# State-space parameter work of a decoder block cut into shorter pieces, all on VectorE, at six points of a pair of feature blocks

## The chip, the cores and the metric

The kernel runs on one core of a Trainium2 chip. The metric is the device time of one execution in microseconds (us), from the profiler's clock of that core; lower is better. Three executions of the kernel before are given, and one more was profiled.

## What is computed

One layer of a decoder block over 1024 tokens of width 1024, in fp32: a SwiGLU feed-forward (inner width 2816), a token mixer (a gated short convolution beside a diagonal state-space scan), a second SwiGLU, and a gated embedding, each followed by a layer norm. Cut to what the change touches:

```python
def swiglu(x, w_in, w_out):
    gate, up = jnp.split(x @ w_in, 2, axis=-1)
    return (jax.nn.silu(gate) * up) @ w_out

def s5_scan(u, lam_re, lam_im, log_step, b_re, b_im, c_re, c_im, d_skip):
    lam = lax.complex(lam_re, lam_im)
    dt = jnp.exp(log_step)[:, None]
    lam_bar = jnp.exp(lam * dt)
    b_bar = ((lam_bar - 1.0) / lam)[..., None] * b_c
...
```

The scan's parameters (powers of lam_bar, b_bar, and the products that the blocked scan multiplies with) depend on small inputs alone. They are computed on the chip while the first feed-forward runs, and stored for the mixer.

## The kernel before, in words

Every fp32 matmul is made of three passes over values split into a high part (fp32r, rounded by ScalarE, L175) and a low part (the rest, subtracted by VectorE, L176). A weight block 128x512 so becomes the tiles Wh and Wl, in a ring of three buffers each.

The first feed-forward (`ffn`, L470) goes through 22 feature blocks, each a `Pair` of a gate half and an up half, over two halves of the tokens. A Winograd scheme needs seven products per pair instead of eight: x11, t1, t2, t3, x21, x22, t4, in that order on TensorE, each of 4 x 3 = 12 matmuls of 512 columns (L198). Three of the seven weight operands come straight from HBM (`Ws`); the other four are sums and differences that GpSimd forms (L79, L84, L88, L96), three of them in the one tile `s` that is written again as soon as its last split has read it. VectorE adds the products in `Pair.rest` (L87, L92, L99, L101, all with one operand in PSUM) and multiplies gate and up (L494, L495). For every second pair GpSimd (L533, L535) and VectorE (L537, L539) also form four sums for the output product.

Between these steps `ffn` draws pieces of a generator, `ssm_prep` (L729): at a point, `tick` runs the generator to its next `yield`, and what it issues is placed after the instruction of that point. The first five pairs have no points. Fifteen pairs have three points each (L87, L99, L495), 45 in all, and the generator has 40 pieces. At the end of the fifteenth the rest of it would be run off, the residual input is loaded (L1155), and the two last pairs and the output product follow.

`ssm_prep` begins with some 150 small operations on 16 to 128 elements per partition (exponentials, sine and cosine, powers; L658 to L807), all on VectorE. Then come four quarters, each with three outer products of complex numbers, `outer`, of 128x512 elements: L, CP and rot, each six operations in `cmul` (L722 to L727, four products, then two sums). L is formed by GpSimd, CP and rot by VectorE. After them TensorE transposes L (L859, 8 transposes), ScalarE scales CP into a block (L846, four operations), and small matmuls (L872, L875) go out through VectorE and ScalarE (L876, L878). The next quarter loads its own small inputs into the one buffer `bc` (L815).

All instructions of an engine run in one order, which the scheduler of the framework writes down from its own estimate of times. So a piece lies on VectorE's queue ahead of or behind the splits that TensorE needs next.

Of the kernel before, what the change touches and what calls it, by code (L numbers as in the profile page):

```python
# [28 lines left out]
class Pair:  # L29
# [43 lines left out]
    def rest(self, tick=lambda ins: None):  # L73
        blk = self.blk
        nc, gps, vec = blk.nc, blk.nc.gpsimd, blk.nc.vector
        u2 = self.u2
        a11, a21, a22 = self.w(0), self.w(0, 1), self.w(1, 1)
        s = blk.t("Ws", [P, 512], name="s")
        gps.tensor_tensor(s, a21, a22, ALU.add)  # L79
        b3 = blk.pm()  # L80
        self.prod(b3, s, "t1")
        p5 = blk.t("T", [P, 512], name="p5")
        nc.scalar.copy(p5, b3)
        gps.tensor_tensor(s, s, a11, ALU.subtract)  # L84
        b2 = blk.pm()
        self.prod(b2, s, "t2")
        tick(vec.tensor_tensor(u2, b2, u2, ALU.add))  # L87
        gps.tensor_tensor(a21, a11, a21, ALU.subtract)  # L88
        b4 = blk.pm()
        self.prod(b4, a21, "t3")  # L90
        u3 = blk.t("T", [P, 512], name="u3")
        vec.tensor_tensor(u3, b4, u2, ALU.add)  # L92
        a12 = self.w(1)
        if not self.early:
            self.second()
        gps.tensor_tensor(s, a12, s, ALU.subtract)  # L96
        self.prod(b3, s, "22", start=False)
        self.a2 = blk.t("H", [P, 512], name="a2")
        tick(vec.tensor_tensor(self.a2, b3, u2, ALU.add))  # L99
        self.prod(b4, a22, "t4", start=False)  # L100
        vec.tensor_tensor(u2, b4, u2, ALU.add)  # L101
        gps.tensor_tensor(u3, u3, p5, ALU.add)  # L102
        self.c1, self.c2 = u2, u3


class Block:
# [363 lines left out]
    def ffn(self, xs, w_in, w_out, acc, after, between, points, begun=(None, None), ahead=None, at=None, early=None):  # L470
        staged, later = begun
        nc = self.nc
# [10 lines left out]
        def products(p):  # L483

            marks = iter(range(points if not p.early else 0))

            def tick(ins):
                if next(marks, None) is not None:
                    with self.tc.issue_after(ins.ins):
                        next(between, None)  # L490

            p.rest(tick)
            nc.scalar.activation(p.a2, p.a2, AF.Silu)
            vec.tensor_tensor(p.a1, p.a1, p.c1, ALU.mult)  # L494
            tick(vec.tensor_tensor(p.a2, p.a2, p.c2, ALU.mult))  # L495
            return p.a1, p.a2

# [154 lines left out]
    def exp_small(self, out, x, n, tmp):  # L652
# [8 lines left out]
        v.scalar_tensor_tensor(r, k, -0.693359375, xc, ALU.mult, ALU.add)  # L661
        v.scalar_tensor_tensor(r, k, 2.12194440e-4, r, ALU.mult, ALU.add)
        v.tensor_scalar(p, r, 1.0 / 5040, None, ALU.mult)
        for c in (1.0 / 720, 1.0 / 120, 1.0 / 24, 1.0 / 6, 0.5, 1.0):
            v.scalar_tensor_tensor(p, p, c, r, ALU.add, ALU.mult)
        v.tensor_scalar(p, p, 1.0, None, ALU.add)
        v.tensor_scalar(k, k, 127.0, None, ALU.add)
        v.tensor_copy(ki, k)
# [3 lines left out]
    def sincos_small(self, sn, cs, x, n):  # L672
# [32 lines left out]
        v.tensor_tensor(c, c, o, ALU.mult)  # L705
        v.tensor_tensor(sn, sn, s, ALU.add)
        v.tensor_tensor(cs, c, w, ALU.add)

        v.tensor_scalar(o, q, 2.0, None, ALU.is_ge)
        v.tensor_scalar(o, o, -2.0, 1.0, ALU.mult, ALU.add)  # L710
# [18 lines left out]
    def ssm_prep(self, prm, dsk, prm_bc):  # L729


        nc = self.nc
        v, gps = nc.vector, nc.gpsimd
        G = 16
        self.scratch = self.carve(self.r("RR", [P, D], 3))
        keep = self.carve(self.r("prm", [P, 368], 1))
# [6 lines left out]
        self.exp_small(dt, lst, G, "e1")  # L743
# [6 lines left out]
        self.exp_small(mag, e2, 2 * G, "e2")  # L750
        yield
        yield from self.sincos_small(sn, cs, th2, 2 * G)
        yield
# [7 lines left out]
        def powers(x, n):  # L761

            v.memset(x[0][:, :, 0:1], 1.0)
            v.memset(x[1][:, :, 0:1], 0.0)
            m = 1
            while m < n:
                br, bi = (y[:, :, m:m + 1].broadcast_to([P, G, m]) for y in x)
                self.cmul(v, x[0][:, :, m + 1:2 * m + 1], x[1][:, :, m + 1:2 * m + 1],
                          x[0][:, :, 1:m + 1], x[1][:, :, 1:m + 1], br, bi, t0[:, :, :m], t1[:, :, :m])
                m *= 2  # L770

        v.tensor_tensor(pw[0][:, :, 1:2], mag[:, :G].unsqueeze(2), cs[:, :G].unsqueeze(2), ALU.mult)
        v.tensor_tensor(pw[1][:, :, 1:2], mag[:, :G].unsqueeze(2), sn[:, :G].unsqueeze(2), ALU.mult)
        powers(pw, 8)
        yield
# [27 lines left out]
        powers(zp, 16)  # L803
        yield
        for ri in range(2):
            v.tensor_copy(wp[ri][:, :, 1:2], zp[ri][:, :, 16:17])
        powers(wp, 8)  # L807
        yield
        for q in range(4):
            g0 = 4 * q  # L810
            gs = slice(g0, g0 + 4)
# [8 lines left out]
            self.cmul(v, bb[0], bb[1], bc[:, 0], bc[:, 1],  # L820
                      *(x[:, gs].unsqueeze(2).broadcast_to([P, 4, 16]) for x in (qr, qi)), t0, t1)

            def outer(eng, dst, x, y):

                xr, xi = (a.unsqueeze(3).broadcast_to(B4) for a in x)
                yr, yi = (a.unsqueeze(2).broadcast_to(B4) for a in y)
                t0, t1 = self.t("T", B4), self.t("T", B4)
                self.cmul(eng, dst[:, 0], dst[:, 1], xr, xi, yr, yi, t0, t1)

            yield  # L830
            L = self.r("RR", [P, 2, 4, 8, 16], 3)
            outer(gps, L, [a[:, gs, 0:8] for a in pw], bb)
            yield
            CP = self.r("RR", [P, 2, 4, 8, 16], 3)
            outer(v, CP, [a[:, gs, 1:9] for a in pw], cc)
            yield

            rot = self.r("RS", [P, 2, 4, 8, 16], 2)
            outer(v, rot, [a[:, gs, 0:8] for a in wp], [a[:, gs, 0:16] for a in zp])
            nc.sync.dma_start(self.rot_d[q], rot.rearrange("p c g a b -> p (c g a b)"))  # L840
            yield

# [297 lines left out]
    def run(self, a, out):  # L1140
# [22 lines left out]
        def then(acc, make, sink):  # L1163
# [3 lines left out]
            def after(s):  # L1167
# [4 lines left out]
                if s % 2:  # L1172
# [4 lines left out]


        state, after = then(acc, self.new_xs, lambda x: self.winograd_sink(x, gbT[0]))
        self.ffn(xs, a["ffn1_w_in"], a["ffn1_w_out"], acc, after, prep(), 3, begun,  # L1180
                 at=19, early=start)

        acc2, last = self.mixer(state["x"], a, acc)
# [129 lines left out]
```

## Time and profile before

| what | value |
|---|---|
| median of 3 runs | 2100.65 us (2095.39 to 2104.41) |
| the profiled execution | 2100.17 us, its span 2098.3 us |
| TensorE busy | 2006.1 us, 96% of the span |
| VectorE busy | 1657.9 us, 79% |
| GpSimd busy | 884.9 us, 42% |
| ScalarE busy | 813.1 us, 39% |
| mean granted TensorE clock | 0.989 of full speed |

The span runs from the first to the last instruction. PE is the matmul side of TensorE, PEld its weight loads, DVE VectorE, ACT ScalarE, POOL GpSimd, SP the engine whose queue issues the DMAs. The generator's pieces lie from about 124 us to 412 us of the span, inside the first feed-forward's pairs.

### The profile page before, as it was taken

The numbers are of one execution on the slowest core, as the hardware profiler recorded it, in microseconds if no ns is written. First come the engines' busy times: TensorE is split into PE (matmuls) and PEld (weight loads), VectorE is DVE, ScalarE is ACT, GpSimd is POOL, SyncE is SP. The second block draws the span as 40 slices with busy tenths as digits, with TensorE's granted clock in tenths as the row PEclk, the third lists the DMA queues.
The fourth block names the chain that finished last, engine by engine and source line by source line (L and its number), as shares of the span: only waits on it lengthen the run. The fifth ranks groups of instructions, "written<-read, shape, count | busy, mean of one in ns | idle before, by whom it ended". The sixth has DMA issues, their size and how long they took to land.

```text
span 2098.3 us, 26462 instructions
## 1 busy us (share of the span) xinstructions
PE 2006.1 (96%) x9030; PEld 1634.8 (78%) x9030; DVE 1657.9 (79%) x2536; ACT 813.1 (39%) x1422; POOL 884.9 (42%) x586
## 2 busy tenths in 40 slices
PE   7998999998999899999999999999999999999988
PEld 5886777786788777888878888788888876788867
DVE  7789768769998976677554678877767689998897
ACT  5323334335442454433543414533333345342520
POOL 4645655545322464333301382664444444313360
PEclk9999999999999999999999999999999999999999
DMA  4432334447441254342483420253333346442111
GB/s 169 129 113 81 123 123 135 155 164 257 149 146 51 110 175 143 104 126 90 136 293 103 134 78 12 69 160 114 100 94 117 100 151 227 157 128 77 50 47 70
DMA packets 153238, 260.24 MB, mean 124 GB/s; under 512 B 16144, under 2 KB 61200, under 8 KB 153104
## 3 DMA queue, kind: packets, MB, share of 16 engines
q1 hardware_dynamic: 153104, 258.56, 38.2%
q8 instruction: 71, 1.16, 0.2%
q14 instruction: 63, 0.52, 0.1%
HBM read 189.85 MB, written 68.65 MB: 123 GB/s over the span
## 4 chain that ended last, share of the span: by engine, by line
PE 65%; DVE 18%; issue 3%; DMA 2%; ACT 1%; POOL 1%; SPq 0%; DVEq 0%; ACTq 0%; POOLq 0%
PE pm L198 39%; PE pm L615 11%; PE pm L209 6%; PE pm L229 5%; DVE Wl L176 3%; PE pm L1234 2%; DVE wt L176 2%; DVE acc L622 1%; DVE w L176 1%; PE pt L1239 1%; DMA Ws<-in_ffn_w_out 1%; DVE ln L254 1%; DVE ln L248 1%; DVE ln L255 1%; DVE acc L316 1%
## 5 line engine op out<-in xcount | busy, mean ns | idle before, releaser
L176 DVE TENSOR_TENSOR Wl<-Ws,Wh 128x512 fp32r<-128x512 f32 x268 | 220.7, 828 | 121.2 <-ACT Wh L175 121.2
L175 ACT CAST Wh<-Ws 128x512 fp32r<-128x512 f32 x268 | 166.6, 622 | 353.4 <-PE pm L198 280.0
L175 ACT CAST Wh<-s 128x512 fp32r<-128x512 f32 x240 | 149.2, 621 | 396.2 <-PE pm L198 143.7
L176 DVE TENSOR_TENSOR Wl<-s,Wh 128x512 fp32r<-128x512 f32 x240 | 214.3, 893 | 28.2 <-ACT Wh L175 28.1
L615 PE MATMUL pm<-wt,Wh 128*128 128x512 f32 x640 | 188.7, 393 | 1.0 <-DVE acc L622 1.0
L84 POOL TENSOR_TENSOR s<-s,Ws 128x512 f32<-128x512 f32 x60 | 87.3, 1456 | 195.8 <-DVE Wl L176 186.4
L102 POOL TENSOR_TENSOR u<-u,p 128x512 f32<-128x512 f32 x60 | 95.1, 1585 | 140.2 <-DVE u L92 98.3
L615 PE MATMUL pm<-w,Wh 128*128 128x512 f32 x480 | 141.2, 392 | 7.7 <-ACT Wh L175 7.2
L622 DVE SCALAR_TENSOR_TENSOR acc<-pm,acc 128x512 f32<-128x512 f32 x200 | 132.6, 682 | 15.6 <-PE pm L615 15.0
L615 PEld LDWEIGHTS pm<-wt,Wh 128*128 128x128 f32 x640 | 120.3, 189 | 28.6 <-DVE acc L622 2.1
L96 POOL TENSOR_TENSOR s<-Ws,s 128x512 f32<-128x512 f32 x60 | 95.0, 1584 | 101.9 <-DVE Wl L176 97.8
L79 POOL TENSOR_TENSOR s<-Ws 128x512 f32<-128x512 f32 x60 | 83.1, 1386 | 124.6 <-DVE Wl L176 109.2
L615 PE MATMUL pm<-wt,Wl 128*128 128x512 f32 x320 | 114.7, 397 | 4.3 <-DVE Wl L176 4.0
L615 PEld LDWEIGHTS pm<-w,Wh 128*128 128x128 f32 x480 | 90.3, 189 | 28.3 <-ACT Wh L175 8.9
L198 PE MATMUL pm<-x21h,Wl 128*128 128x512 f32 x240 | 96.2, 401 | 10.0 <-DVE Wl L176 10.0
L198 PE MATMUL pm<-x11h,Wh 128*128 128x512 f32 (+1 forms) x264 | 98.5, 382 | 4.7 <-ACT x11h L175 4.7
L198 PE MATMUL pm<-xt2h,Wl 128*128 128x512 f32 x240 | 95.6, 398 | 7.0 <-DVE Wl L176 7.0
L198 PE MATMUL pm<-x11h,Wl 128*128 128x512 f32 (+1 forms) x264 | 98.3, 375 | 3.5 <-DVE Wl L176 3.5
L198 PE MATMUL pm<-x11l,Wh 128*128 128x512 f32 (+1 forms) x264 | 98.4, 376 | 2.9 <-DVE x11l L176 2.3
L198 PE MATMUL pm<-xt1h,Wl 128*128 128x512 f32 x240 | 94.9, 396 | 4.6 <-DVE Wl L176 4.6
L198 PE MATMUL pm<-x21h,Wh 128*128 128x512 f32 x240 | 95.6, 398 | 2.1 <-ACT Wh L175 2.1
L198 PE MATMUL pm<-x22h,Wl 128*128 128x512 f32 x240 | 94.0, 392 | 2.6 <-DVE Wl L176 2.5
(367 smaller groups left out, 5637.3 us busy)
## 6 DMA issues: line engine op xcount, KB each, us to landing
Ws<-in_ffn_w_in SPq DMA_DIRECT2D x196, 256.0 KB, 2.7
Ws<-in_ffn_w_out SPq DMA_DIRECT2D x88, 256.0 KB, 3.1
Ws<-in_w_mix SPq DMA_DIRECT2D x74, 256.0 KB, 2.7
s<-h_s SPq DMA_DIRECT2D x60, 256.0 KB, 3.1
h<-a SPq DMA_DIRECT2D x58, 256.0 KB, 2.3
ha<-h SPq DMA_DIRECT2D x20, 512.0 KB, 4.1
hb<-h SPq DMA_DIRECT2D x20, 512.0 KB, 4.7
h_s<-u SPq DMA_DIRECT2D x20, 256.0 KB, 2.6
```

The costliest lines, as they stand in the source:

```text
L79: gps.tensor_tensor(s, a21, a22, ALU.add)
L84: gps.tensor_tensor(s, s, a11, ALU.subtract)
L96: gps.tensor_tensor(s, a12, s, ALU.subtract)
L102: gps.tensor_tensor(u3, u3, p5, ALU.add)
L175: self.nc.scalar.copy(hi, src)
L176: (lo_eng or self.nc.vector).tensor_tensor(lo, src, hi.bitcast(F32), ALU.subtract)
L198: self.nc.tensor.matmul(ps[:, tok], w[a][:, sl], x[b](k)[:, tok], start=(start and k == 0 and i == 0), stop=(k == nk - 1 and i == 2), skip ...
L209: self.nc.tensor.matmul(ps[h], w[a][:, sl], x(h)[b](k), start=(k == 0 and i == 0), stop=(k == 3 and i == 2))
L229: nc.tensor.matmul(ps, a[:, s * P:(s + 1) * P], b[:, cols], start=(j == 0 and i == 0), stop=(j == n - 1 and i == 2))
L615: nc.tensor.matmul(ps[i], hh[p][:, cols], w[n][:, j, q], start=(start and j == 0 and k == 0), stop=(j == 1 and k == 2), skip_group_check=n ...
L622: vec.scalar_tensor_tensor(t, ps[i], scale, t, ALU.mult, ALU.add)
L1234: nc.tensor.matmul(pg, xx[p](k % 4)[:, cols], wg[dh][k][q][:, col], start=(k == 0 and i == 0), stop=(k == NK - 1 and i == 2))
```

## The change

The generator gets more `yield`s: inside the exponentials, the sine and cosine, the powers and the quotient, so that the 8 pieces of small operations become 24 of some five to eight operations; and `outer` no longer calls `cmul`, but issues two products, yields, issues their sum, and does the same for the imaginary part. All three outer products are formed by VectorE. A pair has six points instead of three (L92, L101 and L494 are new), so 90 points for 80 pieces. The number of large operations stays 18 per quarter, 72 in all; 24 of them go from GpSimd to VectorE. The new `outer` names its lines L834, L835 (the two products) and L837 (the sum).

```diff
@@ Pair.rest
-        vec.tensor_tensor(u3, b4, u2, ALU.add)
+        tick(vec.tensor_tensor(u3, b4, u2, ALU.add))
...
-        vec.tensor_tensor(u2, b4, u2, ALU.add)
+        tick(vec.tensor_tensor(u2, b4, u2, ALU.add))
@@ ffn, products
-            vec.tensor_tensor(p.a1, p.a1, p.c1, ALU.mult)
+            tick(vec.tensor_tensor(p.a1, p.a1, p.c1, ALU.mult))
@@ exp_small
         v.tensor_scalar(p, r, 1.0 / 5040, None, ALU.mult)
+        yield
...
@@ powers
                 m *= 2
+                yield
@@ ssm_prep, one quarter
-            def outer(eng, dst, x, y):
+            def outer(dst, x, y):
 
                 xr, xi = (a.unsqueeze(3).broadcast_to(B4) for a in x)
                 yr, yi = (a.unsqueeze(2).broadcast_to(B4) for a in y)
-                t0, t1 = self.t("T", B4), self.t("T", B4)
-                self.cmul(eng, dst[:, 0], dst[:, 1], xr, xi, yr, yi, t0, t1)
+                for i, (p, q), op in ((0, (yr, yi), ALU.subtract), (1, (yi, yr), ALU.add)):
+                    t = self.t("T", B4)
+                    v.tensor_tensor(dst[:, i], xr, p, ALU.mult)
+                    v.tensor_tensor(t, xi, q, ALU.mult)
+                    yield
+                    v.tensor_tensor(dst[:, i], dst[:, i], t, op)
...
-            outer(gps, L, [a[:, gs, 0:8] for a in pw], bb)
+            yield from outer(L, [a[:, gs, 0:8] for a in pw], bb)
...
-            outer(v, CP, [a[:, gs, 1:9] for a in pw], cc)
+            yield from outer(CP, [a[:, gs, 1:9] for a in pw], cc)
...
-            outer(v, rot, [a[:, gs, 0:8] for a in wp], [a[:, gs, 0:16] for a in zp])
+            yield from outer(rot, [a[:, gs, 0:8] for a in wp], [a[:, gs, 0:16] for a in zp])
@@ run
-        self.ffn(xs, a["ffn1_w_in"], a["ffn1_w_out"], acc, after, prep(), 3, begun,
+        self.ffn(xs, a["ffn1_w_in"], a["ffn1_w_out"], acc, after, prep(), 6, begun,
                  at=19, early=start)
```

The order of the instructions differs in the stretch of the generator's pieces; before and behind it, every engine has the order it had.

VectorE, first quarter, from the split of the operand of t1 to that of t2 (`Wl<-s` both times; a_ and u_ are gate and sums of the pair; RR holds L or CP, RS holds rot). Before:

```order
L176 TENSOR_TENSOR Wl<-s,Wh 128x512
L495 TENSOR_TENSOR a_1724<-a_1724,u_1687 128x512
L722 TENSOR_TENSOR RS<-zp 128x512
L723 TENSOR_TENSOR T<-zp 128x512
L724 TENSOR_TENSOR RS<-zp 128x512
L725 TENSOR_TENSOR T<-zp 128x512
L726 TENSOR_TENSOR RR<-RR,T 128x512
L101 TENSOR_TENSOR u_1618<-pm,u_1618 128x512
L727 TENSOR_TENSOR RR<-RR,T 128x512
L726 TENSOR_TENSOR RS<-RS,T 128x512
L176 TENSOR_TENSOR Wl<-s,Wh 128x512
```

And with the change:

```order
L176 TENSOR_TENSOR Wl<-s,Wh 128x512
L495 TENSOR_TENSOR a_1865<-a_1865,u_1824 128x512
L834 TENSOR_TENSOR RR<-prm,bc 128x512
L101 TENSOR_TENSOR u_1754<-pm,u_1754 128x512
L837 TENSOR_TENSOR RR<-RR,T 128x512
L494 TENSOR_TENSOR a_1846<-a_1846,u_1754 128x512
L834 TENSOR_TENSOR RR<-prm,bc 128x512
L835 TENSOR_TENSOR T<-prm,bc 128x512 x2
L176 TENSOR_TENSOR Wl<-s,Wh 128x512
```

Seven large operations of the generator stood between the two splits, five now; ahead of the first split, back to L99, four stood and three stand now. The multiplication L494, which stood behind the second split, now stands ahead of it.

GpSimd, the same quarter's L before, among the operations that form `s` (L84, L96, L79) and the sums (L533, L535):

```order
L84 TENSOR_TENSOR s<-s,Ws 128x512
L533 TENSOR_TENSOR u_1489<-a_1310,a_1526 128x512
L722 TENSOR_TENSOR RR<-prm,bc 128x512
L724 TENSOR_TENSOR RR<-prm,bc 128x512
L535 TENSOR_TENSOR s_1584<-u_1489,a_1291 128x512
L96 TENSOR_TENSOR s<-Ws,s 128x512
L723 TENSOR_TENSOR T<-prm,bc 128x512
L725 TENSOR_TENSOR T<-prm,bc 128x512
L79 TENSOR_TENSOR s<-Ws 128x512
L726 TENSOR_TENSOR RR<-RR,T 128x512
L727 TENSOR_TENSOR RR<-RR,T 128x512
L88 TENSOR_TENSOR Ws<-Ws 128x512
```

With the change:

```order
L84 TENSOR_TENSOR s<-s,Ws 128x512
L533 TENSOR_TENSOR u_1432<-a_1285,a_1475 128x512
L535 TENSOR_TENSOR s_1534<-u_1432,a_1266 128x512
L96 TENSOR_TENSOR s<-Ws,s 128x512
L79 TENSOR_TENSOR s<-Ws 128x512
L88 TENSOR_TENSOR Ws<-Ws 128x512
```

The six operations of L are gone from GpSimd's queue, here and in the three other quarters.

TensorE, the first quarter with the change, from the first two matmuls of t2, which need only Wh, to the third, which is the first to need Wl:

```order
L198 MATMUL pm<-xt2h,Wh 128x512
L198 MATMUL pm<-xt2l,Wh 128x512
L868 MATMUL pt<-ident,RR 128x128 x4
L198 MATMUL pm<-xt3h,Wh 128x512
L198 MATMUL pm<-xt3l,Wh 128x512
L198 MATMUL pm<-xt2h,Wl 128x512
```

Before, two matmuls of t3 and two of x21 stood in this place and no transposes; the eight transposes stood together inside t1. With the change four stand in t1 and four here.

## Rows read from the trace of the kernel before

**Rows 1.** The page: the chain that ended last, share of the span by engine.

```profile
PE 65%; DVE 18%; issue 3%; DMA 2%; ACT 1%; POOL 1%; SPq 0%; DVEq 0%; ACTq 0%; POOLq 0%
```

**Rows 2.** Busy time by stretch: small operations, four quarters, pairs without pieces.

```profile
core 0: us, PE busy (x) PEld busy (x) DVE busy (x) ACT busy (x) POOL busy (x), PEclk, DMA share, GB/s
105.00:199.50 94.50, 87.72 (x372) 69.93 (x371) 84.71 (x236) 27.39 (x48) 51.88 (x34) 0.98 0.34 104
199.50:412.00 212.50, 203.01 (x971) 163.48 (x970) 166.18 (x235) 82.46 (x163) 120.39 (x78) 0.99 0.39 124
412.00:464.00 52.00, 52.00 (x231) 43.07 (x230) 32.06 (x39) 18.15 (x31) 21.65 (x15) 1.00 0.55 183
```

**Rows 3.** Waits from 104 to 470 us: waiter <- releaser: us in total, times, longest.

```profile
PE pm L198 <- DVE Wl L176: 14.1, 10, 4.1
PE pm L198 <- ACT Wh L175: 2.1, 2, 1.6
...
ACT RS L846 <- DVE RR L726: 2.7, 2, 1.3
...
DVE bc L722 <- DMA bc<-in_ssm_bc: 1.2, 1, 1.2
```

**Rows 4.** PE's timeline: start, us, what ran, [idle before, releaser]; six of twelve waits.

```profile
182.40 0.50 PE L198 MATMUL pm<-xt2h,Wl 128*128 128x512 f32 x1 [1.70 <-DVE Wl L176]
...
192.28 0.50 PE L198 MATMUL pm<-x21h,Wl 128*128 128x512 f32 x1 [4.13 <-DVE Wl L176]
...
274.68 0.50 PE L198 MATMUL pm<-xt2h,Wl 128*128 128x512 f32 x1 [2.88 <-DVE Wl L176]
...
320.81 0.50 PE L198 MATMUL pm<-xt2h,Wl 128*128 128x512 f32 x1 [1.71 <-DVE Wl L176]
...
331.00 0.50 PE L198 MATMUL pm<-x22h,Wl 128*128 128x512 f32 x1 [1.55 <-DVE Wl L176]
...
386.28 0.50 PE L198 MATMUL pm<-x21h,Wh 128*128 128x512 f32 x1 [1.57 <-ACT Wh L175]
```

**Rows 5.** Busy time of two short stretches; the column behind POOL's is the granted clock.

```profile
193.40:196.80 3.40, 3.40 (x10) 2.62 (x9) 3.06 (x4) 1.11 (x2) 3.40 (x3) 0.50 0.28 77
275.40:278.80 3.40, 3.40 (x10) 2.62 (x9) 2.71 (x3) 0.35 (x1) 1.52 (x2) 0.51 0.97 319
```

**Rows 6.** POOL's groups of L, 105 to 412 us: busy, mean ns (two of six).

```profile
L724 POOL TENSOR_TENSOR RR<-prm,bc 128x512 f32<-128x512 f32 x4 | 6.9, 1732 | 0.0
...
L725 POOL TENSOR_TENSOR T<-prm,bc 128x512 f32<-128x512 f32 x4 | 5.6, 1392 | 0.0
```

**Rows 7.** POOL's timeline from 181 us, and DVE's at 187 us.

```profile
181.28 2.63 POOL L722 TENSOR_TENSOR RR<-prm,bc 128x512 f32<-128x512 f32 x1 [1.23 <-DVE bc L726]
183.87 2.39 POOL L724 TENSOR_TENSOR RR<-prm,bc 128x512 f32<-128x512 f32 x1
186.22 1.29 POOL L535 TENSOR_TENSOR s<-u,a 128x512 f32<-128x512 f32 x1
...
187.54 1.75 DVE L537 TENSOR_TENSOR s<-a,s 128x512 f32<-128x512 f32 x1 [1.20 <-POOL s L535]
```

**Rows 8.** DVE's timeline, first quarter, between L99 and the split for t2.

```profile
199.22 0.69 DVE L99 TENSOR_TENSOR a<-pm,u 128x512 f32<-128x512 f32 x1 [1.64 <-PE pm L198]
...
201.66 0.68 DVE L725 TENSOR_TENSOR T<-prm,bc 128x512 f32<-128x512 f32 x1
...
203.47 1.77 DVE L722 TENSOR_TENSOR RS<-zp 128x512 f32<-128x512 f32 x1
...
209.37 0.68 DVE L176 TENSOR_TENSOR Wl<-s,Wh 128x512 fp32r<-128x512 f32 x1
```

**Rows 9.** DVE's timeline, second quarter, and POOL's soon after.

```profile
254.79 1.77 DVE L723 TENSOR_TENSOR T<-prm,bc 128x512 f32<-128x512 f32 x1
...
255.98 1.74 POOL L79 TENSOR_TENSOR s<-Ws 128x512 f32<-128x512 f32 x1
```

**Rows 10.** The chain of waits in order of time: the eight transposes.

```profile
205.08 0.87 PE pt L859 x8
```

More of the change, by code (lines that the diff above doesn't have):

```diff
@@ L687, in sincos_small @@
         v.scalar_tensor_tensor(s, s, 1.0, r, ALU.add, ALU.mult)
+        yield
         v.tensor_scalar(c, z, -1.0 / 3628800, None, ALU.mult)
@@ L699, in sincos_small @@
         v.scalar_tensor_tensor(o, q, 3.0, o, ALU.is_equal, ALU.add)
+        yield
         v.tensor_tensor(w, s, o, ALU.mult)
@@ L707, in sincos_small @@
         v.tensor_tensor(cs, c, w, ALU.add)
+        yield
         v.tensor_scalar(o, q, 2.0, None, ALU.is_ge)
@@ L732, in ssm_prep @@
         nc = self.nc
-        v, gps = nc.vector, nc.gpsimd
+        v = nc.vector
         G = 16
@@ L742, in ssm_prep @@
         dt, e2, th2 = self.r1("s_dt", [P, G]), self.r1("s_e2", [P, 2 * G]), self.r1("s_th2", [P, 2 * G])
-        self.exp_small(dt, lst, G, "e1")
+        yield from self.exp_small(dt, lst, G, "e1")
         yield
@@ L749, in ssm_prep @@
         mag, sn, cs = (self.r1(f"s_{i}", [P, 2 * G]) for i in ("mag", "sn", "cs"))
-        self.exp_small(mag, e2, 2 * G, "e2")
+        yield from self.exp_small(mag, e2, 2 * G, "e2")
         yield
@@ L770, in powers @@
                 m *= 2
+                yield
         v.tensor_tensor(pw[0][:, :, 1:2], mag[:, :G].unsqueeze(2), cs[:, :G].unsqueeze(2), ALU.mult)
         v.tensor_tensor(pw[1][:, :, 1:2], mag[:, :G].unsqueeze(2), sn[:, :G].unsqueeze(2), ALU.mult)
-        powers(pw, 8)
-        yield
+        yield from powers(pw, 8)
         den, nr, u0, u1 = (self.r1(f"s_{i}", [P, G]) for i in ("den", "nr", "u0", "u1"))
@@ L786, in ssm_prep @@
         v.tensor_tensor(den, u0, u1, ALU.mult)
+        yield
         l1r, l1i = pw[0][:, :, 1], pw[1][:, :, 1]
@@ L802, in ssm_prep @@
         v.tensor_copy(zp[1][:, :, 1:2], sn[:, G:].unsqueeze(2))
-        powers(zp, 16)
-        yield
+        yield from powers(zp, 16)
         for ri in range(2):
             v.tensor_copy(wp[ri][:, :, 1:2], zp[ri][:, :, 16:17])
-        powers(wp, 8)
-        yield
+        yield from powers(wp, 8)
         for q in range(4):
@@ L821, in ssm_prep @@
                       *(x[:, gs].unsqueeze(2).broadcast_to([P, 4, 16]) for x in (qr, qi)), t0, t1)
-            def outer(eng, dst, x, y):
+            def outer(dst, x, y):
                 xr, xi = (a.unsqueeze(3).broadcast_to(B4) for a in x)
                 yr, yi = (a.unsqueeze(2).broadcast_to(B4) for a in y)
-                t0, t1 = self.t("T", B4), self.t("T", B4)
-                self.cmul(eng, dst[:, 0], dst[:, 1], xr, xi, yr, yi, t0, t1)
+                for i, (p, q), op in ((0, (yr, yi), ALU.subtract), (1, (yi, yr), ALU.add)):
+                    t = self.t("T", B4)
+                    v.tensor_tensor(dst[:, i], xr, p, ALU.mult)
+                    v.tensor_tensor(t, xi, q, ALU.mult)
+                    yield
+                    v.tensor_tensor(dst[:, i], dst[:, i], t, op)
             yield
             L = self.r("RR", [P, 2, 4, 8, 16], 3)
-            outer(gps, L, [a[:, gs, 0:8] for a in pw], bb)
+            yield from outer(L, [a[:, gs, 0:8] for a in pw], bb)
             yield
             CP = self.r("RR", [P, 2, 4, 8, 16], 3)
-            outer(v, CP, [a[:, gs, 1:9] for a in pw], cc)
+            yield from outer(CP, [a[:, gs, 1:9] for a in pw], cc)
             yield
             rot = self.r("RS", [P, 2, 4, 8, 16], 2)
-            outer(v, rot, [a[:, gs, 0:8] for a in wp], [a[:, gs, 0:16] for a in zp])
+            yield from outer(rot, [a[:, gs, 0:8] for a in wp], [a[:, gs, 0:16] for a in zp])
             nc.sync.dma_start(self.rot_d[q], rot.rearrange("p c g a b -> p (c g a b)"))
```

## The prediction

> **What bounds the kernel now.** The chain that ended last comes first: 65% of the span runs over TensorE and 18% over VectorE [rows 1]. So the span is TensorE's matmuls and the gaps between them, and VectorE counts where it makes such a gap. The busy times by stretch come next [rows 2]. In the four quarters TensorE is busy 203.0 of 212.5 us, in the small operations 87.7 of 94.5; in the pairs without pieces behind them 52.0 of 52.0. So the gaps belong to the pieces. VectorE is busy 166.2 of 212.5 us there, 78%, with 46.3 us free: it has room, and the splits are late because of where they stand, not for want of time. The waits say who is late: TensorE waited 14.1 us, in ten waits, for the low part Wl of a split, and 2.1 us in two for Wh [rows 3]; 16.2 us together. The timeline shows when [rows 4]: six waits of 1.55 to 4.13 us make 13.5 of it, the six others 2.7. Two waits, of 4.13 and 2.88 us, were each followed by some 3.4 us at a granted clock of 0.50 and 0.51 [rows 5], the lower of the two levels, 1.2 GHz; half of 3.4 us of matmul work is lost each time, 3.4 us in all. **All that a change here can win is then 16.2 + 3.4 = 19.6 us.** Before 105 us and behind 464 us nothing is moved, and nothing there waits for a clock time of its own: the later work shifts with TensorE.
>
> **The change, part by part.**
>
> *L leaves GpSimd.* Its 24 operations take 1.39 to 1.73 us each in their groups [rows 6], 24 x 1.56 = some 37 us of 172 us that GpSimd is busy in both stretches [rows 2]. They were not on TensorE's path except where a sum stood behind them. At 181 us two of them took 5.0 us ahead of L535; VectorE stood still 1.20 us for its result [rows 7], with the next splits queued behind, and TensorE waited 4.13 us. In the new order nothing stands between L533 and L535. This wait goes, with its clock dip: 4.1 + 1.7 = 5.8 us.
>
> *L comes to VectorE.* An undisturbed 128x512 operation starts 0.60 us after the one before (201.66 to 203.47 holds three of them) [rows 8], so 24 x 0.60 = 14.4 us are added. Against that, an operation with both inputs in SBUF takes 1.77 us where GpSimd works back to back [rows 9], and 0.68 us where it doesn't [rows 8]: 1.09 us more. Taking away 24 GpSimd operations relieves VectorE of between 0 (none met one) and 24 x 1.09 = 26 us. I take the middle, 13 us, since rows of both kinds stand among the twelve operations per quarter. So VectorE's load stays as it was, 78%, with bounds of 155 and 181 us. The Trainium skill's page "SBUF — State Buffer", section "Who interferes with whom", says that a VectorE operation with two SBUF inputs and a GpSimd operation that reads SBUF exclude each other, the later one waiting for the whole of the earlier. By that a meeting would cost up to GpSimd's 1.56 us, so the relief could be 37 us; the rows show 1.09. It also says that the 24 moved operations can block GpSimd's remaining ones.
>
> *Shorter pieces at more points.* What counts is how many operations lie between the end of product x22 (L99) and the split of t2, since t2 is the next operand that must wait for `s` to be rewritten. TensorE needs that Wl after t4, x11, t1 and two matmuls of t2, 38 matmuls; 52.0 us hold 231 of them [rows 2], so 0.225 us each, 8.6 us. In the first quarter VectorE did 15 operations there, from 199.22 to 209.37 us, 10.15 us [rows 8], 15 x 0.60 + 1.09. Now, by the new order, it is 13: 7.8 us, and 8.9, 10.0 or 12.2 with one, two or four of them held up by GpSimd, which has L84, L533, L535 and perhaps L102 to do there. TensorE's own order puts two matmuls of t3 (0.45 us) and eight transposes, 0.87 us [rows 10], before it needs Wl: 9.9 us. So the split is late by 0 to 2.3 us. Counted the same way in the new order, the fourth quarter has 13 operations there too, the third 12, and the second two such places, of 11 and of 9 with six small ones; they are due after 9.0 to 9.9 us. Two meetings at each of the five places make 0.2 us of waiting in all, three make 5, four 10. I take a value between two and three, since the first quarter shows one such meeting and the second a run of them: **3 us left**, bounds 0 and 10.
>
> *ScalarE's four block copies (L846)* stand ahead of a Wh as before; they waited 2.7 us for a sum of CP [rows 3], and 1.57 us of TensorE's waiting is behind that [rows 4]. They stay: **2.1 us left**, bounds 0 and 4.
>
> *Small operations.* 1.70 us at 182.4 us and under 1 us of shorter waits belong to them. Sixteen small operations and two large ones stood before that split; ten and three do now. I leave **0.8 us**, bounds 0 and 2.5.
>
> *DMA and queues.* No transfer is added. `bc` has one buffer and the next load of it is now read sooner; VectorE waited 1.2 us for it once [rows 3]. It may now wait up to three times, with a split behind; two to five us lie between that split and its use, so nothing is added, and 2.5 us is the bound. On SP's queue the new store positions leave the weight loads where they were to within a few issues.
>
> *Sum.* 16.2 - 3 - 2.1 - 0.8 = 10.3 us of waits gone; both clock dips gone, since no wait as long as 2.88 us is left, 3.4 us. 13.7 us. The profiled execution took 2100.17 us, 0.48 below the median of 2100.65; against the median, 2100.65 - 13.7 = **2087.0 us**.
>
> **The rivals.**
>
> *The waits only move* (chance 0.31). VectorE has as much to do as before, and three of the six points (L101, L494, L495) lie within a few operations, at the pair's end, so three pieces come at once. If four meetings are the rule, 10 us of the late splits, 2.1 of Wh and 1.5 of small operations are left, 13.6 of 16.2, and one long wait keeps its dip (1.7): 2.6 + 1.7 = 4.3 us gained, 2096 us. For it: the bunches in the new order; against: the first quarter had eleven such operations in a run and lost nothing to Wl.
>
> *All of it goes* (0.10): 19.6 us, 2081 us. For it: the pairs without pieces have no gap [rows 2]. Against: ScalarE's copies, which nothing moves.
>
> *VectorE becomes the bound, slower* (0.09). All 24 operations meet GpSimd's, at 0.60 + 1.09 us each, 41 us on an engine with 46 us free, and GpSimd's L84 and L96, held up in turn, bring Wh late too. With eight meetings in the thirteen operations a split comes at 7.8 + 8.7 = 16.5 us against 9.9: 6.6 us late at five places, 33 us; with the 2.9 us of the other waits 35.9 us, where 19.6 are lost now: 2100.65 + 16.3 = 2117 us. It turns to slower from (19.6 - 2.9) / 5 = 3.3 us a place on, five meetings of thirteen. Against: GpSimd has three or four operations there. The Trainium skill's rule on the shared port ("SBUF — State Buffer", "Who interferes with whom") speaks against the change here; the trace agrees that a meeting costs time, 1.77 against 0.68 us [rows 8, 9].
>
> **How the numbers follow.** The forecast has 0.50: it stands for 2083 to 2092. Half a per cent, 10.5 us, is about what a measurement of this kernel can tell from no change; the border lies at 2090.1. Nearly all of the forecast and the case in which all goes lie below it, 0.48 + 0.10 = 0.58 faster. The case in which the waits only move and the forecast's edge give 0.33 for no change, the last rival 0.09 for slower. The range goes from 2080 (all gone, and half a us of spread) to 2100, where nearly nothing is won; it leaves out the slower case and some of the edges.
>
> **What would show it.** Right: in the profile after, TensorE's waits from 104 to 470 us are 4 to 8 us instead of 16.2; no half-clock stretch follows 190 or 275 us; the stretch of the quarters is 8 to 10 us shorter; VectorE is busy there about as long as before, GpSimd some 30 us less; L834 to L837 take about 0.7 us on most calls. Wrong: waits for Wl of 2 us and more before t2's third matmul, L834 to L837 near 1.5 us on average, or any wait of TensorE for a transpose's input (RR).

## The result, and the profile after

The changed kernel takes **2086.64 us** (median of 6 runs, 2084.61 to 2087.99), beside 2097.46 us of the kernel before on the same chip. The ratio is **0.9942**, 95% interval 0.9930 to 0.9955: 12 us faster by the ratio, 10.8 by the two medians. The profiled execution took 2086.58 us, its span is 2084.8 us, 13.5 less than before.

The first matmul of the out products (L615) closes the stretch with the parameter work. It starts at 481.26 us of the span before and at 467.64 after, 13.6 us earlier; from there to the end it is 1617.0 and 1617.2 us. So the whole gain lies ahead of it. The chain that ended last, by engine, shows no new owner beside [rows 1]:

```profile
PE 67%; DVE 21%; issue 5%; DMA 2%; ACT 2%; POOL 2%; SPq 0%; DVEq 0%; POOLq 0%; ACTq 0%
```

Busy time by stretch, with the columns of [rows 2]; the first line is the kernel before from 105 us until TensorE has to wait for its out products:

```profile
105.00:478.49 373.49, 357.21 (x1633) 288.14 (x1631) 293.86 (x520) 135.41 (x255) 202.78 (x132) 0.99 0.41 131
```

and the second the kernel after, over the same work:

```profile
105.00:464.88 359.88, 353.17 (x1636) 286.61 (x1634) 302.89 (x544) 136.18 (x256) 166.91 (x109) 1.00 0.42 136
```

The stretch is 13.6 us shorter. VectorE has 24 instructions more and 9.0 us more to do (84% instead of 79% of the stretch), GpSimd 23 fewer and 35.9 us less. The waits after, from 104 to 465 us, answer to [rows 3]:

```profile
PE pm L198 <- DVE Wl L176: 6.5, 9, 1.3
...
ACT RS L869 <- DMA bd<-RS: 5.6, 3, 2.1
...
DVE gp L876 <- DMA gd<-gp: 5.1, 3, 2.9
...
DVE bc L728 <- DMA bc<-in_ssm_bc: 3.6, 2, 2.8
```

TensorE waited 6.5 us where it had waited 16.2, never over 1.31 us, and no longer for Wh. The waits of VectorE and ScalarE for small stores and loads have grown (the second and third line were none, the fourth 1.2 us), probably since the pieces come closer together, and TensorE waits behind none of them. On PE's timeline the four longest waits of the quarters, behind 200 us, stand where three pieces meet at a pair's end (t2) or one precedes a split (t4), to compare with [rows 4]:

```profile
222.53 0.50 PE L198 MATMUL pm<-xt2h,Wl 128*128 128x512 f32 x1 [1.31 <-DVE Wl L176]
...
265.13 0.50 PE L198 MATMUL pm<-xt2h,Wl 128*128 128x512 f32 x1 [0.65 <-DVE Wl L176]
278.24 0.50 PE L198 MATMUL pm<-xt4h,Wl 128*128 128x512 f32 x1 [1.07 <-DVE Wl L176]
...
372.68 0.50 PE L198 MATMUL pm<-xt2h,Wl 128*128 128x512 f32 x1 [1.27 <-DVE Wl L176]
```

Both half-clock stretches of [rows 5] are gone; the granted clock (behind POOL's column) is 1.00 where they stood:

```profile
180.00:200.00 20.00, 18.86 (x83) 15.26 (x83) 19.79 (x58) 5.75 (x11) 10.11 (x6) 1.00 0.37 119
215.00:285.00 70.00, 66.48 (x316) 53.10 (x315) 62.40 (x88) 28.48 (x54) 31.01 (x20) 1.00 0.40 127
```

The groups of the outer products on VectorE (busy, mean ns):

```profile
L837 DVE TENSOR_TENSOR RR<-RR,T 128x512 f32<-128x512 f32 x16 | 15.0, 936 | 0.0
L834 DVE TENSOR_TENSOR RR<-prm,bc 128x512 f32<-128x512 f32 x16 | 14.3, 891 | 0.0
L835 DVE TENSOR_TENSOR T<-prm,bc 128x512 f32<-128x512 f32 x16 | 14.0, 887 | 0.0
L834 DVE TENSOR_TENSOR RS<-zp 128x512 f32<-128x512 f32 x8 | 8.1, 1014 | 0.0
```

0.89 to 1.01 us lies between an undisturbed operation (0.68) and one that meets GpSimd (1.77): 51 of the 72 operations of L834 to L837 took under 0.8 us.

### The profile page after: what moved, and what is told of

The parts are those of the page before. It is cut to its first block, busy times and chain, and to the rows that moved or that the text cites. A ratio compares the mean times of both kernels' runs of the same rounds, so it can differ in the third digit from the quotient of the medians.

```text
span 2084.8 us, 26465 instructions
## 1 busy us (share of the span) xinstructions
PE 2001.7 (96%) x9030; PEld 1633.4 (78%) x9030; DVE 1668.0 (80%) x2560; ACT 813.7 (39%) x1422; POOL 846.4 (41%) x562
## 3 DMA queue, kind: packets, MB, share of 16 engines
q8 instruction: 71, 1.16, 0.2%
## 4 chain that ended last, share of the span: by engine, by line
PE 67%; DVE 21%; issue 5%; DMA 2%; ACT 2%; POOL 2%; SPq 0%; DVEq 0%; POOLq 0%; ACTq 0%
PE pm L198 42%; PE pm L615 11%; PE pm L209 5%; PE pm L229 5%; DVE Wl L176 4%; PE pm L1243 2%; DVE wt L176 2%; DVE w L176 1%; DVE acc L622 1%; DVE ln L254 1%; PE pt L1248 1%; DVE ln L248 1%; DVE ln L255 1%; DVE acc L316 1%; DVE acc L234 1%
## 5 line engine op out<-in xcount | busy, mean ns | idle before, releaser
L176 DVE TENSOR_TENSOR Wl<-Ws,Wh 128x512 fp32r<-128x512 f32 x268 | 212.8, 799 | 109.1 <-ACT Wh L175 108.7
L615 PE MATMUL pm<-wt,Wh 128*128 128x512 f32 x640 | 188.0, 392 | 2.5 <-DVE acc L622 2.5
L84 POOL TENSOR_TENSOR s<-s,Ws 128x512 f32<-128x512 f32 x60 | 90.2, 1503 | 203.6 <-DVE Wl L176 193.3
L615 PE MATMUL pm<-w,Wh 128*128 128x512 f32 x480 | 141.4, 392 | 6.1 <-ACT Wh L175 5.5
L615 PEld LDWEIGHTS pm<-wt,Wh 128*128 128x128 f32 x640 | 119.7, 188 | 30.2 <-DVE acc L622 3.3
L79 POOL TENSOR_TENSOR s<-Ws 128x512 f32<-128x512 f32 x60 | 82.5, 1374 | 133.8 <-DVE Wl L176 102.0
L96 POOL TENSOR_TENSOR s<-Ws,s 128x512 f32<-128x512 f32 x60 | 92.3, 1538 | 108.8 <-DVE Wl L176 107.4
L615 PE MATMUL pm<-wt,Wl 128*128 128x512 f32 x320 | 113.8, 394 | 3.9 <-DVE Wl L176 3.6
L615 PEld LDWEIGHTS pm<-w,Wh 128*128 128x128 f32 x480 | 90.0, 189 | 26.8 <-ACT Wh L175 7.1
L198 PE MATMUL pm<-xt4h,Wl 128*128 128x512 f32 x240 | 94.1, 392 | 4.6 <-DVE Wl L176 4.6
L198 PE MATMUL pm<-xt1l,Wh 128*128 128x512 f32 x240 | 94.4, 393 | 2.1 <-DVE xt1l L176 2.1
```

The source lines that it names most:

```text
L176: (lo_eng or self.nc.vector).tensor_tensor(lo, src, hi.bitcast(F32), ALU.subtract)
L198: self.nc.tensor.matmul(ps[:, tok], w[a][:, sl], x[b](k)[:, tok], start=(start and k == 0 and i == 0), stop=(k == nk - 1 and i == 2), skip ...
L615: nc.tensor.matmul(ps[i], hh[p][:, cols], w[n][:, j, q], start=(start and j == 0 and k == 0), stop=(j == 1 and k == 2), skip_group_check=n ...
```

## The experiments

The change does three things at once: L goes from GpSimd to VectorE, pieces get shorter, and points are added. The table has all runs; "waits" are TensorE's, added up from its timeline between 100 us and the out products, and "clock" is what half-clock stretches cost there (their length times one minus the granted clock). Each is one profiled execution, while the ratio comes from all timed runs.

| kernel | ratio (95%) | waits | clock |
|---|---|---|---|
| before | 1 | 16.2 | 3.4 |
| the change | 0.9942 (0.9930 to 0.9955) | 6.5 | 0 |
| coarse_L_on_vector | 1.0018 (1.0007 to 1.0028) | 17.6 | 5.1 |
| fine_L_on_gpsimd | 0.9977 (0.9967 to 0.9987) | 11.3 | 3.4 |
| fine_three_points | 0.9940 (0.9927 to 0.9953) | 7.5 | 0 |
| coarse_six_points_L_on_vector | 1.0049 (1.0037 to 1.0061) | 24.0 | 6.8 |
| outer_whole_small_short | 1.0000 (0.9991 to 1.0009) | 14.1 | 6.8 |
| outer_short_small_whole | 0.9987 (0.9978 to 0.9996) | 14.6 | 1.7 |
| five_points | 0.9947 (0.9935 to 0.9960) | 3.7 | 0 |
| point_moved_to_split | 0.9934 (0.9922 to 0.9947) | 5.1 | 0 |
| coarse_L_on_vector_spread_points | 0.9969 (0.9957 to 0.9980) | 11.0 | 0 |
| coarse_L_on_vector_sums_on_vector | 0.9959 (0.9947 to 0.9972) | 11.5 | 3.4 |
| after_sums_on_vector | 0.9897 (0.9881 to 0.9913) | 1.9 | 0 |
| before_sums_on_vector | 0.9994 (0.9985 to 1.0003) | 15.6 | 8.5 |

### One part at a time

**coarse_L_on_vector**: the kernel before, with

```diff
-            outer(gps, L, [a[:, gs, 0:8] for a in pw], bb)
+            outer(v, L, [a[:, gs, 0:8] for a in pw], bb)
```

> The kernel before with one word changed: the six large operations of L run on VectorE instead of GpSimd; pieces stay long and the points stay three per pair. My theory (both halves of the change matter): the wait of 4.13 us at 192 us and the two half-clock stretches go, but six operations of 0.9 us in one piece (some 5.5 us) delay the splits behind them, so the stretch keeps 10 to 18 us of TensorE waits on Wl; 2093 to 2101 us, ratio 0.998 to 1.002. Rival A (all of the gain is taking L off GpSimd): 2085 to 2089 us, ratio about 0.994. Rival B (all of the gain is the shorter pieces at more points): no gain at all, 2097 us or more, with waits longer than 16 us in sum.

Slightly slower than before. The ratio is in my theory's range, but the parts are not: half-clock stretches came at other places, 5.1 us of them, where I had none. The wait of 4.13 us is gone, and others took its place, five of them, 7.5 us in sum, for ScalarE's Wh. PE's timeline shows two of those in the first quarter:

```profile
204.64 0.50 PE L198 MATMUL pm<-xt2h,Wh 128*128 128x512 f32 x1 [1.41 <-ACT Wh L175]
207.46 0.80 PE L198 MATMUL pm<-x21h,Wh 128*128 128x512 f32 x1 [1.56 <-ACT Wh L175]
```

ScalarE's cast had waited 7.12 us for the weight sum L84, which GpSimd's timeline shows at three times its usual length:

```profile
199.27 4.67 POOL L84 TENSOR_TENSOR s<-s,Ws 128x512 f32<-128x512 f32 x1 [4.84 <-DVE Wl L176]
```

and VectorE's timeline has two long pieces side by side there, without a pause and each operation at its undisturbed 0.68 us:

```profile
199.12 0.68 DVE L495 TENSOR_TENSOR a<-a,u 128x512 f32<-128x512 f32 x1
199.72 0.68 DVE L722 TENSOR_TENSOR RS<-zp 128x512 f32<-128x512 f32 x1
...
202.12 0.68 DVE L726 TENSOR_TENSOR RR<-RR,T 128x512 f32<-128x512 f32 x1
202.73 0.68 DVE L101 TENSOR_TENSOR u<-pm,u 128x512 f32<-128x512 f32 x1
203.33 1.16 DVE L727 TENSOR_TENSOR RR<-RR,T 128x512 f32<-128x512 f32 x1
```

The sum ends at 203.94, just after L101, the first operation of the row that has an input in PSUM. (The cast behind the second wait also stood behind two of ScalarE's block copies, L846, 1.27 us from 205.49.) The fourth quarter repeats it: L84 4.67 us from 376.84; in each of the two others one sum took 4.36 and 4.68 us. So VectorE's meetings got cheaper (its busy time over the stretch is 292.65 us, 1.2 less than before, with L's 24 operations more), and GpSimd's sums paid for it.

**fine_L_on_gpsimd**: the changed kernel, with

```diff
-            def outer(dst, x, y):
+            def outer(dst, x, y, v=v):
...
-            yield from outer(L, [a[:, gs, 0:8] for a in pw], bb)
+            yield from outer(L, [a[:, gs, 0:8] for a in pw], bb, nc.gpsimd)
```

> The changed kernel with L's operations put back on GpSimd, still in pieces of two products and one sum, at six points of a pair. My theory: the weight sums on GpSimd queue behind at most two of L's operations (about 3.1 us by 1732 and 1392 ns) where they queued behind six, so waits on Wl of 1 to 3 us stay at the four quarters; 2089 to 2093 us, ratio 0.996 to 0.998; GpSimd busy some 30 us longer than in the changed kernel, VectorE some 10 us less. Rival A: all of the gain is lost, 2096 to 2098 us. Rival B: all of it stays, 2085 to 2088 us.

The ratio is as the first theory had it. On GpSimd's timeline in the second quarter, two of L's sums stand ahead of L535:

```profile
267.68 3.45 POOL L837 TENSOR_TENSOR RR<-RR,T 128x512 f32<-128x512 f32 x2
271.09 1.28 POOL L535 TENSOR_TENSOR s<-u,a 128x512 f32<-128x512 f32 x1
```

VectorE stands still for it,

```profile
272.40 1.77 DVE L537 TENSOR_TENSOR s<-a,s 128x512 f32<-128x512 f32 x1 [2.43 <-POOL s L535]
```

and TensorE then waits 1.73 and 1.69 us at 277.12 and 280.01, with a clock stretch behind. This is the chain of [rows 7] again, with a shorter piece. The parts do not add: L's move alone +0.18%, short pieces alone -0.23%, both -0.58%.

**fine_three_points**: the changed kernel without the points behind L92, L101 and L494; `tick` draws twice.

```diff
-        tick(vec.tensor_tensor(u3, b4, u2, ALU.add))
+        vec.tensor_tensor(u3, b4, u2, ALU.add)
...
                         next(between, None)
+                        if points == 6:
+                            next(between, None)
```

> The changed kernel with the three points of a pair that it had before, each drawing two of the short pieces, so that the same work per pair stands in three bunches. My theory: each bunch is two pieces (some 3.5 to 5 us on VectorE), so waits on Wl and pm of 10 to 14 us come back, where the changed kernel has 6.5; 2089 to 2094 us, ratio 0.996 to 0.998. Rival A (only L's engine matters): 2085 to 2088 us as the changed kernel. Rival B (pieces and points are all): 2094 to 2098 us.

No difference from the change: my expectation missed. The number of points is not what pays. The cut is: beside coarse_L_on_vector, which has the same three points, L on the same engine and its pieces in as many pairs, only the cut differs, with the order of operations that comes with it (two short pieces hold three to five large operations of an outer product, a long one six). TensorE's waits before 200 us are 1.3 us instead of 5.4, those behind 6.3 instead of 12.3. Between L99 and the split for t2 stand nine, eight and nine of the generator's large operations in the first, third and fourth quarter, and eleven in each there. (GpSimd's L84 took 4.35 us at 256.00 us here too, and no wait of TensorE stands behind it: a sum that is held up need not cost anything.)

**coarse_six_points_L_on_vector**: the kernel before with L on VectorE and six points, pieces long.

```diff
-            outer(gps, L, [a[:, gs, 0:8] for a in pw], bb)
+            outer(v, L, [a[:, gs, 0:8] for a in pw], bb)
...
-        vec.tensor_tensor(u3, b4, u2, ALU.add)
+        tick(vec.tensor_tensor(u3, b4, u2, ALU.add))
...
-        self.ffn(xs, a["ffn1_w_in"], a["ffn1_w_out"], acc, after, prep(), 3, begun,
+        self.ffn(xs, a["ffn1_w_in"], a["ffn1_w_out"], acc, after, prep(), 6, begun,
```

(and `tick` on L101 and L494 in the same way).

> The kernel before with L on VectorE and a point at six places of a pair, pieces left long (six large operations of an outer product in one). My theory: twice the pieces per pair while they last, each some 5.5 us, so the waits are the longest of all: 16 to 30 us of TensorE waits in the stretch, ended by VectorE; 2096 to 2110 us, ratio 0.999 to 1.006. Rival A: 2085 to 2089 us. Rival B (points as such give the gain): 2088 to 2093 us.

The slowest of all. In one place GpSimd's L96 hardly ran at all; its timeline:

```profile
162.28 9.66 POOL L96 TENSOR_TENSOR s<-Ws,s 128x512 f32<-128x512 f32 x1 [3.21 <-DVE Wl L176]
```

and ScalarE's, behind it:

```profile
171.97 0.62 ACT L175 CAST Wh<-s 128x512 fp32r<-128x512 f32 x1 [10.72 <-POOL s L96]
```

VectorE went from 162.12 to 170.70 us without a pause and without an operand in PSUM; L87, which has one, came at 170.70, and L96 ended at 171.94.

### Which pieces

**outer_whole_small_short** is the changed kernel without the `yield` inside `outer`:

```diff
                     v.tensor_tensor(t, xi, q, ALU.mult)
-                    yield
```

**outer_short_small_whole** keeps that one and leaves out the new ones of the exponential, sine, powers and division, for instance

```diff
-        yield from powers(zp, 16)
+        powers(zp, 16)
+        yield
```

> The changed kernel (L on VectorE, six points), but each outer product is one piece of six large operations again; the small operations stay in short pieces. Theory 1 (it is the length of the outer products' pieces, some 5.3 us by six of 0.9 us, that gave the waits of the run with L on VectorE in long pieces): no TensorE wait above 0.7 us before 200 us of the span, 12 to 20 us of waits behind it, half-clock stretches back; 2096 to 2106 us, ratio 0.999 to 1.004. Theory 2 (the pieces of small operations are as much of it): 2090 to 2094 us, ratio 0.996 to 0.998.

> The changed kernel, but the exponentials, sines, powers and the division stand in their old long pieces; the outer products stay in pieces of two products and one sum. Theory 1: only the waits in the stretch before 200 us come back, two to four of 1.5 to 3 us at 160 to 195 us as in the runs with long pieces (2.75 at 181 and 1.64 at 191.5 there), perhaps with one half-clock stretch of 1.7 us; 2089 to 2093 us, ratio 0.996 to 0.9975. Theory 2: 2092 to 2096 us. If the small pieces do not matter: 2086 to 2088 us.

With whole outer products no wait before 200 us is over 0.61 us, and 12.5 us come behind it, as the first theory said. With whole small work 9.0 us of waits come before 200 us and 5.6 behind: nearly as dear, which the second theory had. With six points both halves of the shortening are needed: without one the change gives 0.58% less, without the other 0.45%. In both kernels six points hand out whole pieces, so that the same work also stands in fewer pairs; these two runs do not separate that from a piece's length.

### The place of the points

**five_points** drops the point behind L101; **point_moved_to_split** puts it behind the split for the product 22:

```diff
         self.prod(b3, s, "22", start=False)
+        tick(blk.last)
...
-        tick(vec.tensor_tensor(u2, b4, u2, ALU.add))
+        vec.tensor_tensor(u2, b4, u2, ALU.add)
```

(`blk.last` is the split's VectorE instruction.)

> The changed kernel without the point behind L101, so that between L99 and t2's split one piece of some 1.8 us less stands on VectorE. If the waits left for t2's weights (1.31, 0.65 and 1.27 us) come from that bunch, they fall under 0.5 us each and the time is 2084 to 2086 us, ratio 0.993 to 0.994. If the bunch is not what delays them (the run with three points of two pieces each was as fast as the change), the sum stays at 6 to 8 us and the time at 2086 to 2088 us.

> The changed kernel with the point behind L101 moved to behind the split for the product 22, so that six pieces a pair stand evenly over the pair. By the bunch as cause of the waits for t2: these fall under 0.5 us each, the split behind 22 may be late by up to 1 us at a few places; 2083 to 2086 us, ratio 0.992 to 0.994. If a piece between 22's split and t4's split costs as much there: 2086 to 2089 us, with the waits moved to t4.

Inconclusive: both intervals overlap the change's. With five points t2 waits once, 0.44 us, and the waits of the stretch are 3.7 us instead of 6.5, but the out products' first wait grows from 2.76 to 4.82 us. Fifteen pairs of five points are 75 for 80 pieces, so the last pieces come late: SP's queue starts the loads of the residual input behind them at 441.63 us, not 406.38, among the loads for the out products, and ScalarE waits 2.32 and 1.36 us for those, with the change 1.69. That this is the reason is likely, not tested. The moved point leaves t2's wait in the first quarter at 1.10 us.

### Testing the blocked sum

If rows of VectorE operations that keep GpSimd's sums from running make the long pieces dear, then breaking the rows, or taking the sums off GpSimd, must help with long pieces too. **coarse_L_on_vector_spread_points** moves the three points of coarse_L_on_vector to L87, L92 and L99, behind three operations that read PSUM (three are drawn, so L495 draws none):

```diff
-        vec.tensor_tensor(u3, b4, u2, ALU.add)
+        tick(vec.tensor_tensor(u3, b4, u2, ALU.add))
```

The two **sums_on_vector** kernels put L84 and L96 of all pairs behind the first five on VectorE (17 pairs, 34 sums, where my expectations counted 16 and 32):

```diff
-        gps.tensor_tensor(s, s, a11, ALU.subtract)
+        add = vec if self.on_vector else gps
+        add.tensor_tensor(s, s, a11, ALU.subtract)
...
-        gps.tensor_tensor(s, a12, s, ALU.subtract)
+        add.tensor_tensor(s, a12, s, ALU.subtract)
```

> The run with L on VectorE in long pieces, its three points moved from L87, L99, L495 to L87, L92, L99, so that no two long pieces stand side by side between L99 and the next split of t2. Theory 1 (a row of VectorE operations on SBUF keeps GpSimd's weight sum from running, as in that run where L84 took 4.67 us twice beside two pieces of six): with one piece between two operations that read PSUM no GpSimd sum takes more than 4 us, the four waits for ScalarE's Wh of 1.0 to 2.0 us go and the half-clock stretch at 384 us with them; 2090 to 2097 us, ratio 0.996 to 0.999. Theory 2 (only the length of one piece in VectorE's own queue counts): 2099 to 2105 us as that run.

> The run with L on VectorE in long pieces, and the weight sums L84 and L96 of the pairs that carry the parameter work (16 pairs, 32 operations of 0.68 us, some 22 us) also on VectorE. Theory 1 (GpSimd's sum is kept waiting by rows of VectorE operations, and ScalarE's cast and TensorE behind it): the waits of TensorE for ScalarE's Wh go, VectorE has 22 us more of its own and 10 to 20 us less from meetings; 2092 to 2100 us, ratio 0.997 to 1.001. Theory 2 (VectorE's own queue is what is late): the added 22 us make the waits on Wl longer, 2104 to 2115 us, ratio above 1.0025.

> The changed kernel with the weight sums L84 and L96 of the same 16 pairs on VectorE: 22 us more there, GpSimd 55 us less, so some 15 to 25 of the operations of 1.2 to 1.8 us should fall back to 0.68 us. Theory 1: VectorE's busy time in the stretch stays within 10 us of the changed kernel's 303 us, waits of 4 to 9 us; 2083 to 2090 us, ratio 0.992 to 0.997. Theory 2: the waits double, 2090 to 2098 us.

Spread, the same long pieces on the same engine take 1.0018 to 0.9969. GpSimd's longest operation of the stretch is now

```profile
176.64 2.49 POOL L84 TENSOR_TENSOR s<-s,Ws 128x512 f32<-128x512 f32 x1 [6.38 <-DVE Wl L176]
```

and one wait for Wh, of 0.65 us, is left of five, while those for Wl went from 8.5 to 10.3 us and VectorE's busy time from 292.65 to 296.80. This speaks for the sums, but does not settle it: the moved points also leave six of the generator's large operations between L99 and the split for t2, where eleven stood in three of the quarters.

With the sums on VectorE the time falls a little further than I had said, and not for the reason that I gave: three waits for Wh stay (3.51, 1.72, 2.15 us), 7.4 us where 7.5 were. At the second the sum stands in VectorE's own row. At the two others it had ended 1.4 us ahead of its cast, which stood behind ScalarE's block copies; VectorE's timeline and ScalarE's at the first:

```profile
201.99 0.68 DVE L86 TENSOR_TENSOR s<-s,Ws 128x512 f32<-128x512 f32 x1
```

```profile
200.91 2.55 ACT L849 ACTIVATE RS<-RR 64x512 f32<-64x512 f32 x4 [2.21 <-DVE RR L729]
203.48 0.58 ACT L84 COPY p<-pm 128x512 f32<-128x512 f32 x1
204.09 0.62 ACT L177 CAST Wh<-s 128x512 fp32r<-128x512 f32 x1
```

What fell are the waits for Wl, from 8.5 to 3.7 us. With 34 operations more, at 0.60 us some 20 us, VectorE's busy time in the stretch fell from 292.65 to 284.67 us: 29 of its operations of 128x512 took over 1 us, where 52 had. So it is shown that rows on VectorE hold GpSimd's sums up, and that breaking the rows ends that; that the held-up sums are what makes the long pieces dear is not.

On the changed kernel the same move is **the fastest version, 2079.78 us**, 0.9897 of before, below both ranges that I had given; its interval lies clear of the change's. The stretch, and TensorE's waits in it:

```profile
105.00:457.05 352.05, 349.96 (x1633) 286.97 (x1632) 296.00 (x578) 136.30 (x255) 110.97 (x74) 1.00 0.43 138
```

```profile
PE pm L200 <- DVE Wl L178: 1.9, 2, 1.6
```

VectorE is busy 296.00 us where the change has 302.89, with the 34 sums more; 39 of its operations of 128x512 took over 1 us instead of 57. GpSimd has 56 us less.

**before_sums_on_vector** is the same edit on the kernel before:

> The kernel before (L on GpSimd, long pieces, three points), with the weight sums L84 and L96 of the same 16 pairs on VectorE. By step (b) of the prediction, the wait of 4.13 us at 192 us is a weight sum queued behind L's operations: with the sums on VectorE it and the half-clock stretch behind it go, though L stays where it was. Theory 1 (the sums' place decides): waits of 6 to 12 us in the stretch, 2086 to 2094 us, ratio 0.994 to 0.9975. Theory 2 (L's meetings with VectorE are what is late): VectorE has 22 us more beside the same L, 2098 to 2110 us.

A miss: no difference. Its profiled execution was the longest of 13 (2107.31 us; the median is 2097.73), yet it shows why. L, on GpSimd, still stands beside the splits. GpSimd's timeline and then VectorE's, while L runs:

```profile
181.72 1.50 POOL L726 TENSOR_TENSOR T<-prm,bc 128x512 f32<-128x512 f32 x1
183.19 1.50 POOL L728 TENSOR_TENSOR T<-prm,bc 128x512 f32<-128x512 f32 x1
184.65 1.34 POOL L729 TENSOR_TENSOR RR<-RR,T 128x512 f32<-128x512 f32 x1
185.95 1.71 POOL L730 TENSOR_TENSOR RR<-RR,T 128x512 f32<-128x512 f32 x1
```

```profile
180.76 1.54 DVE L178 TENSOR_TENSOR Wl<-s,Wh 128x512 fp32r<-128x512 f32 x1
182.23 1.54 DVE L497 TENSOR_TENSOR a<-a,u 128x512 f32<-128x512 f32 x1
...
184.76 1.77 DVE L542 TENSOR_TENSOR a<-a,s 128x512 f32<-128x512 f32 x1
186.46 1.74 DVE L178 TENSOR_TENSOR Wl<-Ws,Wh 128x512 fp32r<-128x512 f32 x1
```

TensorE waits 2.96 and 2.29 us for those two splits. The kernel before has the same meeting in the split that ended its wait of 4.13 us:

```profile
190.68 1.54 DVE L176 TENSOR_TENSOR Wl<-Ws,Wh 128x512 fp32r<-128x512 f32 x1
```

So that wait was L's in two ways, the queue ahead of L535 and the meetings; taking the sums away helps in neither. VectorE's busy time fell here too, from 293.86 to 288.11 us, and the time did not: a less busy VectorE alone is no gain.

## Why the prediction was right, step by step

- *What can be won, 19.6 us*: 9.7 us of waits and 3.4 us of clock were, 13.1 us, which is nearly the 13.6 by which the stretch is shorter.
- *L leaves GpSimd, 5.8 us*: the wait and its clock stretch went, and fine_L_on_gpsimd brings the chain back, in the second quarter. But by itself the step is worth nothing: coarse_L_on_vector has it and is slower. I priced by itself what only holds together with the shorter pieces.
- *L comes to VectorE, load unchanged*: mis-sized. 14.4 us came and 5.4 went, 13 being forecast: +9.0 us, within the bounds. With long pieces the load did stay (-1.2 us); short pieces seem to let GpSimd in more often, at VectorE's cost, and so do spread points (+4.2 us against the same pieces unspread). The term was not in the sum.
- *Shorter pieces at more points, 3 us left*: 4.8 are (1.31, 0.46, 0.65, 1.07, 1.27), two of them at t4, where I had not counted. My count for t2 held: in the first quarter the 13 operations took 10.5 us (211.28 to 221.79), three of them held up, where I had 10.0 for two and 12.2 for four. That the cut pays is shown; "at more points" was wrong, three points do as well.
- *L846 (now L855), 2.1 us left*: nothing was; no wait for Wh remains. *Small operations, 0.8 left*: 1.7 are (0.28, 0.32, 0.47, 0.67). These errors nearly cancel, so that 6.5 us are left where 5.9 were forecast: the sum is closer than its terms, by luck.
- *bc and the queues, nothing*: VectorE's waits for bc grew to 3.6 us in two waits, and no wait of TensorE lies behind them.
- *The rivals*: the mechanism named in "VectorE becomes the bound", L84 and L96 held up in turn and Wh late, did come, in coarse_L_on_vector and coarse_six_points_L_on_vector, which are slower than before. In the change no wait for Wh is left. That waits only move is what coarse_L_on_vector did.
- *The time itself*: 2087.0 was forecast and 2086.64 measured, which is luck in part. I took 13.7 us from 2100.65, the median of three executions; from the median of six, 2097.46, the same sum gives 2083.8. The gain is 13.6 us in the stretch of the two profiles, 12 by the ratio and 10.8 by the medians.

## What to carry to other kernels

Where VectorE and GpSimd both work on SBUF, moving work from one to the other changes the speed of both: cost the pair of engines, not the one. Break long rows of SBUF operations on VectorE into short pieces between operations that read PSUM, above all where GpSimd makes something that ScalarE or TensorE waits for. When GpSimd's operation is short and on the way to a matmul, putting it on a nearly full VectorE can still pay: 34 sums more made VectorE's busy time 7 to 8 us shorter, and the kernel faster, in the two kernels that had L on VectorE. Do not judge by busy time alone: VectorE is busier with the change, 302.89 us, than in the kernel before and in every slower version here (at most 299.29).

## What the runs showed of the hardware

**A GpSimd operation of 1.3 to 1.7 us can take 9.66 us.** In the three places named it ran on until VectorE came to an operation with a PSUM input, and the next one on SBUF was then the slower (1.16 us behind L101). The Trainium skill's page "SBUF — State Buffer", section "Who interferes with whom", says that whichever of the two issues first keeps the shared ports for its whole instruction. The trace agrees that one blocks the other, and adds that a gap between two VectorE operations that follow each other at 0.60 us did not let GpSimd in.

**The length of one wait does not tell whether the clock falls.** In coarse_L_on_vector the granted clock stays at the upper level after a wait of 2.75 us at 181.00. It falls at about 207 us, within the second of two waits of 1.41 and 1.56 us with little work between, and after the out products' 2.75 us at 482.89:

```profile
181.00:184.40 3.40, 3.29 (x13) 2.41 (x14) 3.40 (x6) 0.62 (x1) 1.72 (x1) 1.00 0.23 77
207.40:210.80 3.40, 3.34 (x9) 2.69 (x10) 1.77 (x3) 1.84 (x4) 1.43 (x3) 0.57 0.39 136
482.80:486.20 3.40, 3.31 (x9) 2.62 (x10) 3.40 (x6) 1.79 (x4) 2.24 (x2) 0.59 0.96 381
```

The out products' wait, 2.77 and 2.76 us in the kernels before and after, cost neither of them its clock. A third stretch of the kernel before (0.75 from 520.2 to 527.0 us) went with the two forecast, and another came instead, 0.79 from 703 to 711 us after, which is why the part behind the out products' start takes as long as before. Even from 30 to 42 us, ahead of all that the change moves, the granted clock was 0.72 before and 0.86 after. A forecast that gives each clock stretch to one wait, as mine did, can be off by 1.7 us a place.
